# HGRN2 block scores on the tensor engine: two products of 64 keys by 64 queries in the two column halves of the array, in place of one of 128 by 128

## The chip, the cores and the metric

The kernel runs on one core of one Trainium2 chip. A core has five engines that run side by side and wait for each other through semaphores: the tensor engine (PE, with its weight loads listed as PEld), the vector engine (DVE), the scalar engine (ACT), GpSimd (POOL) and the sync engine (SP), whose queue issues most of the transfers from memory. Matrix products read SBUF and write PSUM, where a tile of this kernel is one bank (2 KB in each of 128 partitions). The metric is the device time of one execution in microseconds, smaller being better.

## What is computed

One decoder layer on 256 tokens of width 1024 in float32. One input projection feeds two token mixers, HGRN2 (a gated linear recurrence) and MoBA attention; their outputs are merged by gates and projected, and a SwiGLU feed-forward follows, each with a residual and a layer norm. The change is in HGRN2, which for each of 8 heads computes

```python
log_f = jnp.logaddexp(jnp.log(lb), jnp.log1p(-lb) + jax.nn.log_sigmoid(z))
k = (1.0 - lb) * jax.nn.sigmoid(-z)
...
diff = G[:, :, :, None, :] - G[:, :, None, :, :]          # G = cumsum of log_f
decay = jnp.exp(jnp.where(causal, diff, -jnp.inf))
scores = jnp.einsum('bhtsd,bhtd,bhsd->bhts', decay, qc, kc)
o = jnp.einsum('bhts,bhsv->bhtv', scores, vc) + jnp.einsum('bhtd,bhdv->bhtv', qc * jnp.exp(G), state)
```

The score of a query at token t and a key at token s is a sum over 128 channels d of q, k and the product of the forget gates between s and t, which differs from channel to channel.

## The kernel before

**The levels.** The kernel holds keys and queries with the 128 channels on the partitions and all 256 tokens of 8 heads along the free axis, in two halves `u` of 128 tokens (the second half runs backwards, `ORDER`). It computes the scores in `hgrn_steps` (line 491) by doubling blocks. At level `l` (line 522), with `n = 2**l`, the tokens stand in blocks of `n`, and blocks are paired: a later block of queries against the earlier block of keys beside it. Queries `Qt` and keys `Kt` carry the gates of their blocks already, so a score between the two blocks is a plain product over channels. The views `earlier` (line 485) and `later` (line 488) pick the earlier blocks of keys and the later blocks of queries of both token halves, 128 of each per head.

A level has four parts:

- ACT copies the earlier keys of all 8 heads into the contiguous tile `KL` (line 535; the pool `klp` has one buffer, so the copy for the next level waits until the products of this one have read it).
- PE multiplies, for each head, 128 keys by 128 queries into PSUM (line 543), four heads to a bank, two banks `sc{l}_{g}` a level. The operands are float32, and each such product runs as two matmul instructions with a weight load each: 16 matmul instructions a level. Of the 128 by 128 scores only those between a block and its own partner are wanted. The rest is computed and dropped.
- For blocks under 32 tokens (levels 1 to 4) DVE copies the wanted scores under a mask into `SD` (line 554), once per bank. For blocks of 32 and 64 tokens (levels 5 and 6, `n >= BLOCKS`) ACT copies the wanted rectangles (line 551), 8 copies at level 5 and 4 at level 6.
- DVE multiplies queries (line 560) and keys (line 561) by the gates of the neighbouring block for the next level, and halves the table of gate products (line 564).

Level 0 is different: a product of one key by one query is a sum over partitions, made with a matrix of ones (line 540). It is left as it is. After level 6 come the products between the two token halves (line 572), and then the outputs (line 584).

**What runs around them.** The levels are one step list, `side`, that is advanced between the projections of `hg`, `mv` and `gb` (`tok_chunk`, lines 387 to 389). Each half of such a projection uses one weight tile of 1 MB: SP issues its load (line 220), ACT rounds it (`wh`, line 221), DVE takes the rest (`wl`, line 223), and PE multiplies it in 24 matmuls. There are four buffers each of `wh` and `wl`.

**The order.** In this part of the kernel the order on each engine is not written out: a planner simulates the program and places each instruction when its inputs are ready by its own estimate of times (`schedule_with_timeline_sim=True`, line 1149). Only the start (line 411), the stretch around the output projection (line 903) and the end (line 976) are in an order written out by hand. An engine executes its instructions in the planned order and waits at one whose input isn't there.

Of the kernel before, what the change touches and what calls it, by code (L numbers as in the profile page):

```python
# [10 lines left out]
F32 = mybir.dt.float32  # L11
# [6 lines left out]
P = 128  # L18
T = 256
NT = T // P  # L20
D = 1024
KC = D // P
H = 8
# [103 lines left out]
def hybrid_layer_kernel(ctx: ExitStack, tc, x, xw, vecs, bias, wts, ln1_w, ln1_b, ln2_w, ln2_b, consts, out):  # L127
    nc = tc.nc
# [9 lines left out]
    aux = pool("aux", 4, space=PSUM)  # L138
# [4 lines left out]
    def r32(ap):  # L143
        return ap.bitcast(F32)
# [152 lines left out]
    masks = cst[:, C_MASK:C_END].bitcast(U32).rearrange("p (l t) -> p l t", l=LEVELS)  # L297
# [158 lines left out]
    for j in range(4):  # L456
        sg = sm.tile([P, 2, T], F32, tag="sg", name=f"sgq{j}")
        sgs = [by_half(sg[:, f, :]) for f in range(2)]
        if j < HQ_WIDE:
            for f, ps in enumerate(wide_pair(f"hq{j}", xp, mm, "mm")):  # L460
                z = Qg[:, :, 2 * j + f, :]
# [3 lines left out]
        else:  # L465
            ps = feat_pair(f"hq{j}")
            nc.scalar.activation(sg, ps, AF.Sigmoid)
            qs = [by_half(ps[:, f, :]) for f in range(2)]
        for f in range(2):
            h = 2 * j + f  # L470
# [9 lines left out]
    def free_view(ap, offset, dims):  # L480
        return bass.AP(ap.tensor, ap.offset + offset, [ap.ap[0]] + dims)
# [6 lines left out]
    def later(z, n, h0=0, nh=H):  # L488
        return free_view(z, h0 * P + n, [[P, nh], [2 * n, 64 // n], [H * P - n, NT], [1, n]])

    def hgrn_steps():
        Qt, SD = halves(slot("Qt")), halves(slot("SD"))
        Tt = slot("Tt")
        nc.vector.tensor_mul(Qt, Qg, Fg)


        up, down = slice(0, P // 2), slice(P // 2, P)
        kq, half_sum, kqp = slot("kq"), slot("hs"), slot("kqp", F32R)

        def fold(dst, src, cols, a, b):  # L500

            s = half_sum[a, cols]
            nc.scalar.copy(s, src[b, :])
            nc.vector.tensor_add(s, src[a, :], s)
            nc.scalar.copy(dst[a, :], s)
            nc.vector.tensor_sub(dst[b, :], s, r32(dst[a, :]))

        flat = lambda z: z.rearrange("p u h t -> p (u h t)")
        nc.vector.tensor_mul(kq, flat(Kt), flat(Qg))
        fold(kqp, kq, slice(0, 2048), up, down)  # L510
        yield
        for g in range(4):
            ps = aux.tile([P, 4, P], F32, tag="aux", name=f"sd{g}")
            cs = slice(g * 512, (g + 1) * 512)
            row = ps.rearrange("p h t -> p (h t)")
            nc.tensor.matmul(row, ones, kqp[:, cs], start=True, stop=True)
            nc.vector.tensor_tensor(SD[:, g // 2, 4 * (g % 2):4 * (g % 2) + 4, :], ps,
                                    ident[:, None, :].to_broadcast([P, 4, P]), op=ALU.mult)
        yield
        tot, size = Fg, NT * H * P  # L520
        off = 0
        for l in range(LEVELS):
            n = 2 ** l
            nb = 64 // n
            flat = lambda z: z.rearrange("p h b u i -> p (h b) u i")
            if l == 0:

                pr = klp.tile([P, H * P], F32, tag="kl", name="pr")
                prp = slot("prp", F32R)[:, 0:H * P]
                nc.vector.tensor_mul(pr.rearrange("p (a u i) -> p a u i", u=NT, i=n),  # L530
                                     flat(later(Qt, n)), flat(earlier(Kt, n)))
                fold(prp, pr, slice(0, H * P), down, up)
            else:
                KL = klp.tile([P, H, P], F32, tag="kl", name=f"kl{l}")
                nc.scalar.copy(KL.rearrange("p h (b u i) -> p h b u i", u=NT, i=n), earlier(Kt, n))
            for g in range(2):
                ps = aux.tile([P, 4, P], F32, tag="aux", name=f"sc{l}_{g}")
                if l == 0:
                    row, cs = ps.rearrange("p h t -> p (h t)"), slice(g * 512, (g + 1) * 512)
                    nc.tensor.matmul(row, ones, prp[:, cs], start=True, stop=True)  # L540
                for a in range(4 if l > 0 else 0):
                    h = 4 * g + a
                    nc.tensor.matmul(ps[:, a, :], KL[:, h, :], later(Qt, n, h, 1), start=True, stop=True)  # L543
                if n >= BLOCKS:

                    for b in range(nb):
                        for u in range(NT):
                            r0 = (2 * b + u) * n
                            c0 = 2 * b * n + (1 - u) * n
                            rows = slice(r0, r0 + n)  # L550
                            nc.scalar.copy(SD[rows, u, 4 * g:4 * g + 4, c0:c0 + n], ps[rows, :, r0:r0 + n])
                    continue
                m = masks[:, l, :].rearrange("p (b u i) -> p b u i", u=NT, i=n)
                nc.vector.copy_predicated(later(SD, n, 4 * g, 4),
                                          m[:, None, :, :, :].to_broadcast([P, 4, nb, NT, n]),
                                          ps.rearrange("p a (b u i) -> p a b u i", u=NT, i=n))

            first = free_view(tot, 0, [[2, H * nb], [size // NT + 1, NT], [0, n]])
            second = free_view(tot, 1, [[2, H * nb], [size // NT - 1, NT], [0, n]])
            nc.vector.tensor_mul(flat(later(Qt, n)), flat(later(Qt, n)), first)  # L560
            nc.vector.tensor_mul(flat(earlier(Kt, n)), flat(earlier(Kt, n)), second)
            if l < LEVELS - 1:
                nxt = Tt[:, off:off + size // 2]
                nc.vector.tensor_mul(nxt, free_view(tot, 0, [[2, size // 2]]), free_view(tot, 1, [[2, size // 2]]))
                off += size // 2
                tot, size = nxt, size // 2
            yield
        SL = klp.tile([P, H, P], F32, tag="kl", name="SL")
        for g in range(2):
            ps = aux.tile([P, 4, P], F32, tag="aux", name=f"sc7_{g}")  # L570
            for a in range(4):
                nc.tensor.matmul(ps[:, a, :], Kt[:, 0, 4 * g + a, :], Qt[:, 1, 4 * g + a, :], start=True, stop=True)
            nc.scalar.copy(SL[:, 4 * g:4 * g + 4, :], ps)
        yield
        on = slot("on").rearrange("p (t d) -> p t d", t=NT)
        for g in range(2):
            for u in range(NT):
                ps = aux.tile([P, 4, P], F32, tag="aux", name=f"o{g}{u}")
                for a in range(4):
                    h = 4 * g + a  # L580
                    hd = slice(h * P, (h + 1) * P)
                    if u == 1:
                        nc.tensor.matmul(ps[:, a, :], SL[:, h, :], hv[:, 0, hd], start=True, stop=False)
                    nc.tensor.matmul(ps[:, a, :], SD[:, u, h, :], hv[:, u, hd], start=(u == 0), stop=True)
                sq = sm.tile([P, 4, P], F32, tag="sg", name=f"sq{g}{u}")
                nc.scalar.activation(sq, ps, AF.Square)
                st = sm.tile([P, 12], F32, tag="ost", name=f"ost{g}{u}")
                nc.vector.reduce_sum(st[:, 0:4], sq, axis=mybir.AxisListType.X)
                nc.vector.tensor_scalar(st[:, 4:8], st[:, 0:4], 1.0 / P, RMS_EPS, op0=ALU.mult, op1=ALU.add)  # L589
                nc.gpsimd.tensor_tensor(st[:, 8:12], st[:, 4:8], half, op=ALU.pow)  # L590
                for a in range(4):
                    hd = slice((4 * g + a) * P, (4 * g + a + 1) * P)
                    nc.vector.scalar_tensor_tensor(on[:, u, hd], ps[:, a, :], st[:, 8 + a:9 + a], hgs[:, u, hd],
                                                   op0=ALU.mult, op1=ALU.mult)
            yield
            for j in range(2):
                h0 = 4 * g + 2 * j
                pt = aux.tile([P, 2, T], F32, tag="aux", name=f"ot{g}{j}")
                for a in range(2):
                    for u in range(NT):  # L600
                        hd = slice((h0 + a) * P, (h0 + a + 1) * P)
                        nc.tensor.transpose(pt[:, a, u * P:(u + 1) * P], on[:, u, hd], ident)
                for a in range(2):
                    h = h0 + a
                    nc.scalar.activation(yah[:, h, :], pt[:, a, :], AF.Copy, scale=nw[:, h:h + 1])
                    nc.vector.scalar_tensor_tensor(yal[:, h, :], pt[:, a, :], nw[:, h:h + 1], r32(yah[:, h, :]),
                                                   op0=ALU.mult, op1=ALU.subtract)
        yield
# [367 lines left out]
    with tc.manual_schedule(engines={ET.PE, ET.DVE, ET.Activation}):  # L976
# [56 lines left out]
        z, spare = [slot("z")[:, i:i + D] for i in (0, D)]  # L1033
# [8 lines left out]
        for i, (raw, (k0, wh, wl)) in enumerate(zip(last_raw, held)):  # L1042
# [5 lines left out]
            c = sums[:, 2 * i:2 * i + 2].unsqueeze(2).to_broadcast([P, 2, SUMS])  # L1048
# [106 lines left out]
```

## Time and profile before

| | |
|---|---|
| runs of the kernel (3) | 492.78, 493.17, 493.47 us; median 493.17 us |
| span of the profiled execution, first to last instruction | 491.2 us |
| instructions in the span | 6768 |
| mean granted clock of the tensor engine | 0.996 |
| data moved | 99.99 MB, mean 204 GB/s |
| products of the six levels (line 543) | 96 matmul instructions, first start at 91.0 us, last at 135.6 us |

The span is that of one execution taken by the hardware profiler. No time of its own is listed for that execution outside the profile, so the span stands for it: the 2.0 us between it and the median of the runs lie around the first and the last instruction. In rows of a timeline, the first two numbers are the start and the length in microseconds; in rows of groups, `xN` is the number of instructions, followed by the busy time in us and the mean of one in ns. A matmul's length contains its way through the array, so neighbouring matmuls overlap in time; the pace is read from the distance between starts.

### The profile page before, as it was taken

What the parts mean: (1) busy time and instruction counts of PE and PEld (TensorE: products, weight loads), DVE (VectorE), ACT (ScalarE), POOL (GpSimd) and SP (SyncE); (2) the same over time, 40 slices, a digit from 0 to 9 for tenths busy, and PEclk for the clock granted to TensorE, in tenths of its full rate; (3) what the DMA queues carried; (4) which work ended last, traced back from release to release, by engine and by line L of the source; (5) the groups of instructions that cost most, each with busy time, mean ns of one, the idle gap of its engine ahead of it and who ended that gap; (6) DMA issues with size and microseconds to landing.
All of it is one profiled execution on the core that took longest, in us unless ns stands there. A gap on an engine that the chain in (4) does not pass through costs nothing.

```text
span 491.2 us, 6768 instructions
## 1 busy us (share of the span) xinstructions
PE 484.2 (99%) x2621; PEld 418.4 (85%) x2621; DVE 406.7 (83%) x523; ACT 293.7 (60%) x410; POOL 39.6 (8%) x46
## 2 busy tenths in 40 slices
PE   9999999999999999999999999999999999999994
PEld 9889888888899888988888888888888888888784
DVE  4979899999767979999675678856797878989996
ACT  5797587435755767775843462544655655576673
POOL 0000000000003431250000000000000000000030
PEclk9999999999999999999999999999999999999998
DMA  8987426635442437248545446257869644266852
GB/s 301 418 312 251 172 95 248 229 157 171 172 171 87 131 135 293 107 154 292 220 163 183 168 183 230 103 180 275 314 218 335 218 173 173 90 233 243 315 149 85
DMA packets 17631, 99.99 MB, mean 204 GB/s; under 512 B 1984, under 2 KB 3776, under 8 KB 7616
## 3 DMA queue, kind: packets, MB, share of 16 engines
q1 hardware_dynamic: 14400, 92.62, 51.6%
q0 software_dynamic: 3056, 6.82, 4.3%
q8 instruction: 20, 0.33, 0.3%
q10 hardware_dynamic: 144, 0.13, 0.1%
q14 instruction: 11, 0.09, 0.1%
HBM read 94.84 MB, written 3.15 MB: 199 GB/s over the span
## 4 chain that ended last, share of the span: by engine, by line
PE 90%; DVE 5%; issue 2%; ACT 1%; DMA 1%; DVEq 0%; POOLq 0%; POOL 0%; ACTq 0%
PE fu L336 7%; PE fg L336 7%; PE fg L338 3%; PE fu L338 3%; PE mq L336 2%; PE mk L336 2%; PE hq L336 2%; PE sc L543 2%; PE hf L361 2%; PE za L387 1%; PE ga L387 1%; PE za L388 1%; PE ga L388 1%; PE ga L389 1%; PE za L389 1%
## 5 line engine op out<-in xcount | busy, mean ns | idle before, releaser
L223 DVE TENSOR_TENSOR wl<-raw,wh 128x2048 fp32r<-128x2048 f32 (+1 forms) x71 | 164.9, 2328 | 47.4 <-ACT wh L221 46.9
L221 ACT CAST wh<-raw 128x2048 fp32r<-128x2048 f32 (+1 forms) x71 | 133.6, 1887 | 64.4 <-PE fg L336 13.5
L336 PE MATMUL fg<-x1p,wh 128*128 128x512 f32 x144 | 50.5, 394 | 0.0
L336 PE MATMUL fu<-x1p,wh 128*128 128x512 f32 x144 | 50.4, 394 | 0.0
L338 PE MATMUL fg<-x1p,wl 128*128 128x256 f32 x144 | 40.0, 278 | 0.0
L338 PE MATMUL fu<-x1p,wl 128*128 128x256 f32 x144 | 39.9, 277 | 0.0
L336 PEld LDWEIGHTS fu<-x1p,wh 128*128 128x128 f32 x144 | 27.0, 187 | 6.2
L336 PEld LDWEIGHTS fg<-x1p,wh 128*128 128x128 f32 x144 | 27.0, 187 | 6.1
L338 PEld LDWEIGHTS fg<-x1p,wl 128*128 128x128 f32 x144 | 27.1, 188 | 0.1
L338 PEld LDWEIGHTS fu<-x1p,wl 128*128 128x128 f32 x144 | 27.1, 188 | 0.0
L336 PE MATMUL mk<-xp,wh 128*128 128x512 f32 x48 | 16.8, 396 | 0.0
L336 PE MATMUL mq<-xp,wh 128*128 128x512 f32 x48 | 16.7, 395 | 0.0
L336 PE MATMUL hq<-xp,wh 128*128 128x512 f32 x48 | 16.7, 394 | 0.0
L590 POOL TENSOR_TENSOR ost<-ost,half 128x4 f32<-128x4 f32 x4 | 4.1, 1014 | 152.6 <-DVE ost L589 152.6
L338 PE MATMUL hq<-xp,wl 128*128 128x256 f32 x48 | 13.3, 277 | 0.0
L338 PE MATMUL mq<-xp,wl 128*128 128x256 f32 x48 | 13.0, 279 | 0.0
L338 PE MATMUL mk<-xp,wl 128*128 128x256 f32 x48 | 13.0, 281 | 0.0
L389 PE MATMUL za<-wl,yah 128*128 128x512 f32 x32 | 12.7, 396 | 0.0
L885 PE MATMUL fe<-wh,x1p 128*128 128x512 f32 x32 | 12.6, 395 | 0.0
L387 PE MATMUL za<-wh,yah 128*128 128x512 f32 x32 | 12.6, 395 | 0.0
L389 PE MATMUL gb<-wl,xp 128*128 128x512 f32 x32 | 12.6, 395 | 0.0
L811 PE MATMUL wo<-wh,mTh 128*128 128x512 f32 x32 | 12.6, 394 | 0.0
(380 smaller groups left out, 1359.5 us busy)
## 6 DMA issues: line engine op xcount, KB each, us to landing
raw<-in_wts_dram SPq DMA_DIRECT2D x69, 1024.0 KB, 4.8
rawcorners<-in_wts_dram SPq DMA_DIRECT2D x5, 1024.0 KB, 4.7
xw<-in_xw_dram SPq DMA_DIRECT2D x6, 640.0 KB, 9.6
rawahead<-in_wts_dram SPq DMA_DIRECT2D x2, 1024.0 KB, 4.8
rawsums<-spill SPq DMA_DIRECT2D x2, 1024.0 KB, 4.7
rawcorners<-in_wts_dram SPq DMA_DIRECT2D x2, 768.0 KB, 5.7
raw<-in_wts_dram SPq DMA_DIRECT2D x2, 512.0 KB, 10.8
xr<-in_x_dram POOLq DMA_DIRECT2D x1, 1024.0 KB, 5.5
```

What stands on the lines that cost most here:

```text
L221: nc.scalar.copy(h[:, ks, :], raw[:, ks, :])
L223: eng.tensor_sub(l[:, ks, :], raw[:, ks, :], r32(h[:, ks, :]))
L336: nc.tensor.matmul(ps, wh[:, k, wcol], a.both(k), start=(k == 0), stop=False)
L338: nc.tensor.matmul(ps[:, 0, :], wl[:, k, wcol], a[0, k, slice(0, T)], start=False, stop=(k == KC - 1))
L361: nc.tensor.matmul(ps, wh[:, kk, wcol], xp.both(k), start=False, stop=False)
L387: nc.tensor.matmul(pss[t], ah[:, kk, ts], wh[:, k, :], start=(kk == 0), stop=False)
L388: nc.tensor.matmul(pss[t], al[:, kk, ts], wh[:, k, :], start=False, stop=False)
L389: nc.tensor.matmul(pss[t], ah[:, kk, ts], wl[:, k, :], start=False, stop=(kk == KC - 1))
L543: nc.tensor.matmul(ps[:, a, :], KL[:, h, :], later(Qt, n, h, 1), start=True, stop=True)
L590: nc.gpsimd.tensor_tensor(st[:, 8:12], st[:, 4:8], half, op=ALU.pow)
L811: nc.tensor.matmul(ps, lh(kk)[:, ts], wh[:, k, ns], start=(kk == first), stop=False)
L885: nc.tensor.matmul(ps, x1p[0, kk, ts], wh[:, k, :], start=(kk == 0), stop=False)
```

## The change

For levels 1 to 6, each head's product of 128 keys by 128 queries is replaced by two products of 64 keys by 64 queries: the keys of one half of `KL`'s columns against the queries that belong to them. The first writes PSUM partitions 0 to 63, the second partitions 64 to 127, of a tile with 64 columns a head, so that the scores of all eight heads lie in one bank in place of two. A block and its partner always lie in the same half (for 64 tokens the half is the token half), so every wanted score is still computed. A level has 32 matmul instructions in place of 16, each with 64 weight columns in place of 128 and 64 moving columns in place of 128.

The masked copy of levels 1 to 4 becomes one instruction for 8 heads in place of two for 4 each; it reads the 64 columns twice, once for each half, under the same mask. The copies of levels 5 and 6 take 8 heads at a time: 4 and 2 in place of 8 and 4. Level 0 keeps two banks and two masked copies.

```diff
+    def later_half(z, n, h, c):
+        if n == 64:
+            return free_view(z, h * P + n + c * (H * P - n), [[1, n]])
+        return free_view(z, h * P + n + c * 64, [[2 * n, 32 // n], [H * P - n, NT], [1, n]])
...
-            for g in range(2):
-                ps = aux.tile([P, 4, P], F32, tag="aux", name=f"sc{l}_{g}")
-                if l == 0:
+            m = masks[:, l, :]
+            if l == 0:
+                for g in range(2):
+                    ps = aux.tile([P, 4, P], F32, tag="aux", name=f"sc{l}_{g}")
                     row, cs = ps.rearrange("p h t -> p (h t)"), slice(g * 512, (g + 1) * 512)
                     nc.tensor.matmul(row, ones, prp[:, cs], start=True, stop=True)
-                for a in range(4 if l > 0 else 0):
-                    h = 4 * g + a
-                    nc.tensor.matmul(ps[:, a, :], KL[:, h, :], later(Qt, n, h, 1), start=True, stop=True)
+                    nc.vector.copy_predicated(later(SD, n, 4 * g, 4),
...
+            else:
+                ps = aux.tile([P, H, 64], F32, tag="aux", name=f"sc{l}")
+                for h in range(H):
+                    for c in range(2):
+                        own = slice(c * 64, (c + 1) * 64)
+                        nc.tensor.matmul(ps[own, h, :], KL[:, h, own], later_half(Qt, n, h, c),
+                                         start=True, stop=True)
                 if n >= BLOCKS:
...
-                            nc.scalar.copy(SD[rows, u, 4 * g:4 * g + 4, c0:c0 + n], ps[rows, :, r0:r0 + n])
-                    continue
-                m = masks[:, l, :].rearrange("p (b u i) -> p b u i", u=NT, i=n)
-                nc.vector.copy_predicated(later(SD, n, 4 * g, 4),
-                                          m[:, None, :, :, :].to_broadcast([P, 4, nb, NT, n]),
-                                          ps.rearrange("p a (b u i) -> p a b u i", u=NT, i=n))
+                            nc.scalar.copy(SD[rows, u, :, c0:c0 + n], ps[rows, :, r0 % 64:r0 % 64 + n])
+                else:
+                    part = [[2 * n, 32 // n], [n, NT], [1, n]]
+                    nc.vector.copy_predicated(
+                        free_view(SD, n, [[P, H], [64, 2], [2 * n, 32 // n], [H * P - n, NT], [1, n]]),
+                        free_view(m, 0, [[0, H], [64, 2]] + part),
+                        free_view(ps, 0, [[64, H], [0, 2]] + part))
```

More of the change, by code (lines that the diff above doesn't have):

```diff
@@ L535, in hgrn_steps @@
                 nc.scalar.copy(KL.rearrange("p h (b u i) -> p h b u i", u=NT, i=n), earlier(Kt, n))
-            for g in range(2):
-                ps = aux.tile([P, 4, P], F32, tag="aux", name=f"sc{l}_{g}")
-                if l == 0:
+            m = masks[:, l, :]
+            if l == 0:
+                for g in range(2):
+                    ps = aux.tile([P, 4, P], F32, tag="aux", name=f"sc{l}_{g}")
                     row, cs = ps.rearrange("p h t -> p (h t)"), slice(g * 512, (g + 1) * 512)
                     nc.tensor.matmul(row, ones, prp[:, cs], start=True, stop=True)
-                for a in range(4 if l > 0 else 0):
-                    h = 4 * g + a
-                    nc.tensor.matmul(ps[:, a, :], KL[:, h, :], later(Qt, n, h, 1), start=True, stop=True)
+                    nc.vector.copy_predicated(later(SD, n, 4 * g, 4),
+                                              m.rearrange("p (b u i) -> p b u i", u=NT, i=n)[:, None, :, :, :]
+                                              .to_broadcast([P, 4, nb, NT, n]),
+                                              ps.rearrange("p a (b u i) -> p a b u i", u=NT, i=n))
+            else:
[5 more added lines that the diff above has]
+                                         start=True, stop=True)
                 if n >= BLOCKS:
```

## The prediction

> **What bounds the kernel now.** I read the page first: the busy shares, the forty slices, then the chain that ended last.
>
> ```profile
> span 491.2 us, 6768 instructions
> ...
> PE 484.2 (99%) x2621; PEld 418.4 (85%) x2621; DVE 406.7 (83%) x523; ACT 293.7 (60%) x410; POOL 39.6 (8%) x46
> ...
> PE   9999999999999999999999999999999999999994
> ...
> DVE  4979899999767979999675678856797878989996
> ...
> PE 90%; DVE 5%; issue 2%; ACT 1%; DMA 1%; DVEq 0%; POOLq 0%; POOL 0%; ACTq 0%
> ```
>
> PE is busy in every slice but the last, and the chain runs over PE for 90% of the span. DVE is as full as PE in slices 6 to 10 (61 to 123 us), which is where the levels are worked out. So I look at the levels by stage: the windows view, cut at the products of levels 2 to 6. The columns are the window, its length, then busy time and count for PE, PEld, DVE, ACT and POOL.
>
> ```profile
> 87.50:102.50 15.00, 15.00 (x83) 13.00 (x83) 14.93 (x14) 6.10 (x6) 0.00 (x0) 1.00 0.62 224
> 102.50:110.60 8.10, 8.10 (x45) 6.88 (x44) 8.00 (x7) 3.46 (x4) 0.00 (x0) 1.00 0.34 131
> 110.60:118.80 8.20, 8.20 (x46) 7.08 (x45) 8.10 (x8) 5.18 (x5) 0.00 (x0) 1.00 0.37 128
> 118.80:127.00 8.20, 8.20 (x46) 7.09 (x45) 7.24 (x8) 3.80 (x4) 0.00 (x0) 1.00 0.72 256
> 127.00:136.00 9.00, 9.00 (x50) 7.74 (x49) 6.14 (x5) 7.15 (x16) 0.00 (x0) 1.00 0.34 118
> ```
>
> PE never idles here; DVE idles 0.3 us up to 118.8 and 3.8 us after. The chain of waits for this stretch (start, length) has the six groups of products:
>
> ```profile
> 91.14 1.92 PE sc L543 x16
> ...
> 100.56 1.78 PE sc L543 x16
> ...
> 108.70 1.84 PE sc L543 x16
> ...
> 116.91 1.78 PE sc L543 x16
> ...
> 125.05 1.78 PE sc L543 x16
> ...
> 134.11 1.78 PE sc L543 x16
> ```
>
> All six are on the chain: 1.92 + 1.84 + 4 x 1.78 = 10.88 us, or 0.111 us for each of 16 instructions at 1.78. The change works on these 10.88 us.
>
> **What the products will cost.** A level gets 32 instructions, each with half the queries. What an instruction of 64 columns costs is seen only at the very start, in the timeline of the warm-up products:
>
> ```profile
> 3.26 0.63 PE L430 MATMUL warm<-const-float32-1.0 128*128 128x128 f32 x2
> ...
> 3.47 0.63 PE L430 MATMUL warm<-const-float32-1.0 128*128 128x128 f32 x2
> ...
> 3.90 0.53 PE L430 MATMUL warm<-const-float32-1.0 128*128 128x64 f32 x2
> 4.00 0.42 PE L430 MATMUL warm<-const-float32-1.0 128*128 128x64 f32 x1
> ```
>
> Starts of 128 columns are 0.21 us apart, those of 64 columns 0.10: half. (The pace of these rows is half that of the levels, 0.111, though the clock column shows 1.00 for them; I use the ratio only.) So 64 columns should take 0.111 / 2 = 0.056 us in the levels, and two products of 64 by 64, one after the other, take what one of 128 by 128 takes: 32 x 0.056 = 1.78 us. **Half the columns alone bring nothing; the gain must come from the two halves of the array working at once.** The ends for a group are
>
> - 0.89 us, if the halves overlap completely (32 x 0.028);
> - 1.78 us, if they don't overlap;
> - 3.5 us, if an instruction with its weight load can't be had faster than 0.109 us, which is the least distance that any row at full pace shows (32 x 0.109); the warm-up rows speak only down to 0.10.
>
> The 0.109 is that of the transposes, by the chain:
>
> ```profile
> 275.80 0.87 PE mt L778 x8
> ```
>
> No row has two products in two halves. The order written in the loop is: half 0 first pass, half 0 second pass, half 1 first pass, half 1 second pass, next head. The two passes of one half can't overlap, neighbours of different halves may. If the later of two neighbours starts a step s after the earlier, a head takes 2 x 0.056 + 2 s, with s between 0 and 0.056. The nearest row, the warm-up, shows columns alone setting the pace, so I stay near that end and take a quarter of the way, s = 0.014: 0.139 us a head, 1.11 us a group. Gain: 10.88 - 6 x 1.11 = **4.2 us** (ends: +5.5 and -10.1; the last is 10.88 - 6 x 3.5).
>
> The Trainium skill's page "TensorEngine Tiling (Array Packing)", section "Tiling Modes", says that different tiles of the array can load weights and multiply in parallel, which is what the gain needs. The page "TensorE: Matmul & The Clock Gate", Part 1, section "Wait — 56ns, not 53.3ns?", speaks against it: starts of matmuls never come closer than about 25 ns. With s = 0.025 a head would take 0.161 us, by an estimate from that page, and the gain would be 3.1 us; no row here has starts that close.
>
> **What the change of shape costs.** All products around the levels use the whole array, so each level now enters and leaves another shape: 12 changes. Before, entering and leaving a group is free:
>
> ```profile
> 124.66 0.39 PE L389 MATMUL gb<-wl,xp 128*128 128x512 f32 x1
> ...
> 124.89 1.95 PE L543 MATMUL sc<-Qt,kl 128*128 128x128 f32 x16
> ...
> 126.59 0.48 PE L387 MATMUL gb<-wh,xp 128*128 128x512 f32 x1
> 126.91 0.40 PE L388 MATMUL gb<-wh,xp 128*128 128x512 f32 x1
> ```
>
> From 124.66 to 126.91 are 2.25 us; two products of 512 take 0.23 each, which leaves 1.79 for the 16. The groups by form say what would show if the array had to run empty between two shapes:
>
> ```profile
> L543 PE MATMUL sc<-Qt,kl 128*128 128x128 f32 x96 | 11.9, 276 | 0.0
> ```
> ```profile
> L543 PEld LDWEIGHTS sc<-Qt,kl x96: 186/192/192, 90.7 to 135.5; 128*128 128x128 f32 x96
> ```
>
> An instruction is 0.276 us long at a pace of 0.111: 0.165 us are its way through, hidden by the next one. Running empty exposes these 0.165 us; a weight load that can't start early adds up to 0.19 us. Ends per change: 0 and 0.36 us. I take 0.165, as the load needs nothing from the array's outputs: 12 x 0.165 = **2.0 us** (0 to 4.3). The same page on tiling says, in "Key Properties", that changing the mode drains the array while changing the tile within a mode doesn't. No row of this trace has a change of shape.
>
> **What is late next.** Of the inputs of a group, the queries come last. From the timeline, DVE's multiply and the first product behind it, levels 2 and 3:
>
> ```profile
> 98.37 1.48 DVE L560 TENSOR_TENSOR Qt<-Qt,Tt 128x1024 f32<-128x1024 f32 x1
> ...
> 100.40 0.27 PE L543 MATMUL sc<-Qt,kl 128*128 128x128 f32 x1
> ```
> ```profile
> 107.17 1.21 DVE L560 TENSOR_TENSOR Qt<-Qt,Tt 128x1024 f32<-128x1024 f32 x1
> ...
> 108.54 0.33 PE L543 MATMUL sc<-Qt,kl 128*128 128x128 f32 x1
> ```
>
> The queries are ready 0.55 us before level 2 and 0.16 us before level 3. DVE is full until then and won't be earlier, while PE comes earlier by (4.2 - 2.0) / 6 = 0.37 us a level: 0.37 at level 2, covered; 0.74 at level 3, of which 0.58 isn't. Behind the waiting product the rest of PE's queue waits. The planner places products by its own times and may put another projection product ahead of them. Ends: 0 and 0.6 us (1.6 with full overlap); I take **0.4 us**. Levels 4 and 6 have 2 us in hand (114.92 against 116.91; for level 6 the keys' copy comes last, 131.66 against 133.94):
>
> ```profile
> 113.71 1.21 DVE L560 TENSOR_TENSOR Qt<-Qt,Tt 128x1024 f32<-128x1024 f32 x1
> ```
> ```profile
> 130.61 1.05 ACT L535 COPY kl<-Kt 128x1024 f32<-128x1024 f32 x1
> ...
> 133.94 1.95 PE L543 MATMUL sc<-Qt,kl 128*128 128x128 f32 x16
> ```
>
>
> Can the weights follow? ACT takes a `wh` buffer as PE frees it:
>
> ```profile
> 116.94 1.91 ACT L221 CAST wh<-raw 128x2048 fp32r<-128x2048 f32 x1 [3.02 <-PE gb L388]
> ```
> ```profile
> 120.55 2.28 DVE L223 TENSOR_TENSOR wl<-raw,wh 128x2048 fp32r<-128x2048 f32 x1
> ```
>
> The buffer freed at 116.9 is complete at 122.8, and PE has three other tiles (24 products of 0.23, 5.5 us each) to go through first: over 10 us in hand, so nothing of a gain of 2 to 5 us is lost there, and SP's loads move with the buffers.
>
> **The copies.** The masked ones, with the least, median and greatest length, and ACT's commoner form:
>
> ```profile
> L554 DVE COPY_PREDICATED SD<-cst,sc x10: 733/744/2527, 91.6 to 118.8; 128x512 f32<-128x512 uint32 x10
> ```
> ```profile
> L551 ACT COPY SD<-sc 32x128 f32<-32x128 f32 x8 | 2.0, 255 | 0.1
> ```
>
> Eight masked copies become four of twice the size: the same elements, four starts fewer, counted as nothing (a few tenths on a full DVE). If the new views went at the pace of level 0's copies (2.5 us for 512 elements, the greatest length), each would take 5 us; this is the upper end, and would push the queries back by some 3 us a level, a cost that case 4 below covers. ACT saves under 1 us, and in the windows above it is busy for 25.7 of 48.5 us: nothing.
>
> **Where the gain arrives.** Near the end DVE carries the chain, but it starts from PE:
>
> ```profile
> 443.91 0.24 PE wp L813
> 444.21 1.92 ACT whsums L266
> ```
>
> So whatever PE gains before 444 us moves the end. Sum on the span: -4.2 + 2.0 + 0.4 = -1.8 us, so 489.4 in place of 491.2. The median of the runs lies 2.0 us above the span; the same difference on it gives 491.4 us.
>
> **The rivals.**
>
> 1. Forecast, 0.43: overlap with a small step, 491.4 us. For it: columns set the pace in every row. Full overlap with free changes would be 10.88 - 5.34 = 5.5 us less, 487.6.
> 2. Overlap eaten up, 0.22: with s half of 0.056 a head takes 0.167 us, a group 1.34, the gain is 2.9; changes of shape take 2.0 and the wait 0.2: -0.7 us, 492.5. It is the rule of the 25 ns that leads here.
> 3. Slower, 0.24: the halves don't work at once, the group stays at 1.78 us, and 12 changes at 0.165 to 0.36 us come on top: +2.0 to +4.3 us, 495.2 to 497.5. The place is the first product behind each change. It decides as soon as a group's gain is under two changes, 0.33 us, so above 1.48 us a group. For it: no row shows overlap, and PE has no idle in which a change could hide. It is also the case in which the change doesn't do what it says.
> 4. Much slower, 0.11: 0.109 us per instruction with its weight load, 32 a level: +10.1 + 2.0 us, 505 us. For it: no row at full pace is faster. Against it: the warm-up halves.
>
> **How the numbers follow.** A measurement of this kernel can tell about 0.2% (1 us) from no change. Case 1 is faster by more (0.43), case 2 within (0.22), cases 3 and 4 slower (0.35). The range has to hold cases 1 to 3 with their unknown ends; case 4 and the last half microsecond at either outer end are left out: 488.0 to 497.0 us. Case 1 by itself spans 488 to 492.
>
> **What would show it.** In the profile after: the chain's groups of line 543 at about 1.1 us for 32 instructions (case 3: 1.8; case 4: 3.5); starts of products in different halves closer than 0.056 us; the first product behind a group late by about 0.17 us at either end; PE idle before level 3 by up to 0.6 us with the queries as releaser; masked copies of levels 3 and 4 near 1.4 us each. The forecast is wrong if the groups don't shrink, if a change of shape costs over 0.35 us, or if the planner's new order leaves PE waiting elsewhere.

## The result and the profile after

The changed kernel takes 490.13 us (median of 4 runs, 489.95 to 490.37) against 493.14 us before: a ratio of 0.9942 with a 95% interval of 0.9928 to 0.9956. It is **3.0 us faster**; 491.4 us (1.8 us faster) was predicted. Two single runs, one of the kernel before at 1258 us and one of the kernel with an extra product at the end of each group at 1249 us, lie far outside all the others and are left out of every ratio in this document. The span of the profiled execution went from 491.2 to 488.5 us.

The page of the changed kernel, busy times and the chain's shares:

```profile
span 488.5 us, 6947 instructions
...
PE 481.0 (98%) x2717; PEld 413.0 (85%) x2717; DVE 404.2 (83%) x519; ACT 292.7 (60%) x404; POOL 38.8 (8%) x46
...
PE 89%; DVE 5%; DMA 2%; issue 2%; ACT 1%; DVEq 0%; POOLq 0%; POOL 0%; SPq 0%; ACTq 0%
```

PE has 96 instructions more (six levels, 16 more each) and is busy 3.2 us less. The picture is the old one otherwise: PE carries the chain. The chain of waits (start, length) shows the six groups, now line 556:

```profile
91.34 1.15 PE sc L556 x32
...
100.66 1.08 PE sc L556 x32
101.74 0.43 PE mv L389
...
108.76 1.08 PE sc L556 x32
109.85 0.43 PE mv L389
...
116.87 1.08 PE sc L556 x32
117.95 0.43 PE gb L389
...
126.56 1.08 PE sc L556 x32
127.65 0.43 PE gb L387
...
134.44 1.08 PE sc L556 x32
```

32 instructions take 1.08 us where 16 took 1.78, and the projection product behind a group takes 0.43 us on the chain in place of 0.23. To see both at once, read a group from the last projection product before it to the second one behind it, in the timeline of the changed kernel:

```profile
116.48 0.39 PE L388 MATMUL gb<-wh,xp 128*128 128x512 f32 x1
116.80 1.15 PE L556 MATMUL sc<-Qt,kl 128*64 128x64 f32 x32
117.88 0.50 PE L389 MATMUL gb<-wl,xp 128*128 128x512 f32 x1
118.22 0.39 PE L387 MATMUL gb<-wh,xp 128*128 128x512 f32 x1
```

From 116.48 to 118.22 are 1.74 us; two projection products take 0.23 each (0.46), which leaves **1.28 us** for a group with its two changes of shape. The same reading gave 1.79 before. Six times 0.51 is 3.1 us, the whole gain; read one by one, the six groups save 0.51 to 0.58 us each, 3.2 us together. All experiments below are read in this way; the number is called the group's net time.

### The profile page after: what moved, and what is told of

Its sections match the earlier page's. It is cut to its first block, busy times and chain, and to the rows that moved or that the text cites. A ratio compares the mean times of both kernels' runs of the same rounds, so it can differ in the third digit from the quotient of the medians.

```text
span 488.5 us, 6947 instructions
## 1 busy us (share of the span) xinstructions
PE 481.0 (98%) x2717; PEld 413.0 (85%) x2717; DVE 404.2 (83%) x519; ACT 292.7 (60%) x404; POOL 38.8 (8%) x46
## 4 chain that ended last, share of the span: by engine, by line
PE 89%; DVE 5%; DMA 2%; issue 2%; ACT 1%; DVEq 0%; POOLq 0%; POOL 0%; SPq 0%; ACTq 0%
PE fu L336 7%; PE fg L336 7%; PE fg L338 3%; PE fu L338 3%; PE mq L336 2%; PE mk L336 2%; PE hq L336 2%; PE mv L389 2%; PE gb L389 2%; PE gb L387 2%; PE hg L387 2%; PE hf L361 2%; PE za L387 2%; PE ga L389 2%; PE ga L387 1%
## 5 line engine op out<-in xcount | busy, mean ns | idle before, releaser
L223 DVE TENSOR_TENSOR wl<-raw,wh 128x2048 fp32r<-128x2048 f32 (+1 forms) x71 | 163.2, 2305 | 44.3 <-ACT wh L221 43.9
L389 PE MATMUL mv<-wl,xp 128*128 128x512 f32 x32 | 12.8, 399 | 0.0
```

The costliest lines, as they stand in the source:

```text
L223: eng.tensor_sub(l[:, ks, :], raw[:, ks, :], r32(h[:, ks, :]))
L389: nc.tensor.matmul(pss[t], ah[:, kk, ts], wl[:, k, :], start=False, stop=(kk == KC - 1))
```

## The experiments

Eight kernels were run. Each is the changed kernel with one edit. Ratios are to the kernel before, which ran beside them.

### Do the two halves really work at once?

Half the columns alone were predicted to bring nothing. To see whether the gain comes from the halves working side by side, the same 32 instructions are issued with neighbours in the same half:

```diff
-                for h in range(H):
-                    for c in range(2):
+                for c in range(2):
+                    for h in range(H):
```

PE's instructions, by line and shape, come in the same order as in the changed kernel, so the order inside the groups is all that differs on PE.

> Same instructions as the changed kernel, but within a level all eight products of the left half come first, then all eight of the right half, so neighbours are in the same half. Overlap theory (the gain comes from neighbours in different halves): starts 0.055 us apart throughout, a group of 32 takes 1.75 to 1.8 us in place of 0.94, plus the same two changes of shape: 490.1 + 6 x 0.83 = 495.1 us, slower than the kernel before. Rival (an instruction with 64 weight columns and 64 moving columns simply costs 0.029 us with its load, whichever half it is in): no change, 490.1 us.

Measured: 494.52 us, ratio 1.0026 (1.0017 to 1.0035), slower than before. Its timeline:

```profile
118.34 0.39 PE L388 MATMUL gb<-wh,xp 128*128 128x512 f32 x1
118.66 1.90 PE L556 MATMUL sc<-Qt,kl 128*64 128x64 f32 x32
120.49 0.50 PE L389 MATMUL gb<-wl,xp 128*128 128x512 f32 x1
120.82 0.39 PE L387 MATMUL gb<-wh,xp 128*128 128x512 f32 x1
```

2.48 - 0.46 = 2.02 us net, 0.74 more than in the changed kernel; six times that is 4.4 us, and the time rose by 4.4 us. The rival (narrow instructions are cheap wherever they stand) is out. A product's half of the array is also its half of the PSUM partitions; no run separates the two. This run is also the price of the prediction's third case: without alternating halves the change would have cost 1.3 us, less than the 2.0 to 4.3 named there, since at the one border the halves still overlap a little.

### How far can a later product run ahead?

The prediction assumed that instructions start strictly in order, so that only neighbours in different halves overlap. Two orders between the extremes test it. The edit is that of two heads in a row; for four heads, the 2 of the step and the 2 of the inner loop are 4:

```diff
-                for h in range(H):
-                    for c in range(2):
-                        own = slice(c * 64, (c + 1) * 64)
...
+                for h, c in [(h0 + a, c) for h0 in range(0, H, 2) for c in range(2) for a in range(2)]:
+                    own = slice(c * 64, (c + 1) * 64)
```

> The changed kernel's products with two heads in a row in the same half: left half heads 0 and 1, right half heads 0 and 1, and so on, so runs of 4 instructions in one half. Strictly in order, only the neighbours at the 7 borders overlap: 32 x 0.0585 - 7 x 0.052 = 1.51 us a group (0.94 with single products), +0.57 a level, 493.5 us. If a later instruction of the other half can start while earlier ones still wait for theirs (in the kernel that takes the halves in turn, three instructions overlap at the one border), three of four overlap at each border: 32 x 0.0585 - 21 x 0.052 = 0.78, so no less than the 0.94 of full overlap, 490.1 us.

> The same with four heads in a row in the same half: runs of 8 instructions, 3 borders. Strictly in order: 32 x 0.0585 - 3 x 0.052 = 1.72 us a group, +0.78 a level, 494.8 us. If three instructions overlap at each border: 1.40 us a group, +0.46 a level, 492.9 us.

Measured: 490.65 us with two heads in a row (ratio 0.9948, 0.9929 to 0.9968), 492.35 us with four (0.9978, 0.9967 to 0.9989). The timelines, two heads in a row and then four:

```profile
116.97 0.39 PE L388 MATMUL gb<-wh,xp 128*128 128x512 f32 x1
117.29 1.20 PE L555 MATMUL sc<-Qt,kl 128*64 128x64 f32 x32
118.42 0.50 PE L389 MATMUL gb<-wl,xp 128*128 128x512 f32 x1
118.76 0.39 PE L387 MATMUL gb<-wh,xp 128*128 128x512 f32 x1
```
```profile
117.59 0.39 PE L388 MATMUL gb<-wh,xp 128*128 128x512 f32 x1
117.90 1.54 PE L555 MATMUL sc<-Qt,kl 128*64 128x64 f32 x32
119.38 0.50 PE L389 MATMUL gb<-wl,xp 128*128 128x512 f32 x1
119.71 0.40 PE L387 MATMUL gb<-wh,xp 128*128 128x512 f32 x1
```

Net 1.33 and 1.66 us. Less 0.35 for the two changes (next experiment) these are 0.98 and 1.31 us of products, below the strict order's 1.51 and 1.72 and beside the other theory's 0.94 and 1.40. The built programs hold the products of a group in the order written. So an instruction of the other half starts while a few before it still wait for theirs. Runs of 4 instructions in one half are nearly free, runs of 8 are not.

### Products and changes of shape, each by itself

Issuing every product of a level twice leaves the two changes as they are and doubles the rest:

```diff
-                for h in range(H):
+                for h in list(range(H)) * 2:
```

> Each level's 16 products are issued twice in a row, 64 instructions between one entry and one exit. If a group is 0.94 us of products (16 neighbours pairs of 0.0585) plus a fixed 0.34 us for entering and leaving the other shape: +0.94 us a level, 490.1 + 5.6 = 495.7 us, and the extra time at the two ends of the group stays as it is. Rival without fixed cost (1.28 us / 32 = 0.040 us an instruction): +1.28 us a level, 497.8 us.

Measured: 496.06 us, ratio 1.0054 (1.0037 to 1.0071).

```profile
117.95 0.39 PE L388 MATMUL gb<-wh,xp 128*128 128x512 f32 x1
118.27 2.08 PE L556 MATMUL sc<-Qt,kl 128*64 128x64 f32 x64
120.28 0.50 PE L389 MATMUL gb<-wl,xp 128*128 128x512 f32 x1
120.62 0.39 PE L387 MATMUL gb<-wh,xp 128*128 128x512 f32 x1
```

2.67 - 0.46 = 2.21 us net for 64 instructions against 1.28 for 32: **0.93 us for 32 instructions, and 0.35 us that don't depend on their number.** The second term by another way: an extra product of 128 by 128 in the middle of a group brings two changes more, the same product at its end none.

```diff
+                wide = aux.tile([P, P], F32, tag="aux", name=f"wide{l}")
                 for h in range(H):
+                    if h == 4:
+                        nc.tensor.matmul(wide, KL[:, h, :], later(Qt, n, h, 1), start=True, stop=True)
```

> The changed kernel with one extra product of 128 keys by 128 queries a level (two instructions, 0.22 us, its result isn't used), put between head 3 and head 4 of each group, so that each level leaves and enters the other shape once more: two more changes a level. If a change costs 0.17 us: +6 x (0.22 + 0.34) = +3.4, 493.5 us, and the instruction behind each change is late as at the ends of the group. If a change costs nothing of itself: +1.3, 491.4 us, the same as with the extra product at the end.

> The changed kernel with the same extra product of 128 keys by 128 queries a level (its result isn't used) behind head 7, where the shape changes anyway: no more changes than before. Both theories: +6 x 0.22 = +1.3, 491.4 us. It is what the kernel with the product in the middle is to be compared with.

Measured: 494.38 us (ratio 1.0029, 1.0020 to 1.0039) in the middle, 492.08 us (0.9982, 0.9972 to 0.9993) at the end. Timelines, middle and end:

```profile
117.61 0.39 PE L389 MATMUL gb<-wl,xp 128*128 128x512 f32 x1
117.93 0.69 PE L559 MATMUL sc<-Qt,kl 128*64 128x64 f32 x16
118.55 0.49 PE L556 MATMUL wide<-Qt,kl 128*128 128x128 f32 x2
118.97 0.69 PE L559 MATMUL sc<-Qt,kl 128*64 128x64 f32 x16
119.58 0.50 PE L387 MATMUL gb<-wh,xp 128*128 128x512 f32 x1
119.92 0.39 PE L388 MATMUL gb<-wh,xp 128*128 128x512 f32 x1
```
```profile
116.67 0.39 PE L388 MATMUL gb<-wh,xp 128*128 128x512 f32 x1
116.99 1.15 PE L557 MATMUL sc<-Qt,kl 128*64 128x64 f32 x32
118.07 0.49 PE L559 MATMUL wide<-Qt,kl 128*128 128x128 f32 x2
118.31 0.48 PE L389 MATMUL gb<-wl,xp 128*128 128x512 f32 x1
118.63 0.39 PE L387 MATMUL gb<-wh,xp 128*128 128x512 f32 x1
```

Net 1.85 and 1.50 us: two changes cost 0.35 us, 0.17 each, and the time differs by 2.3 us where six times 0.35 is 2.1. The product at the end costs 1.50 - 1.28 = 0.22 us a level, as expected, which is 1.3 us; the run was 2.0 us above the changed kernel. The other 0.6 us isn't in the groups and stays open; apart from the one left out, the runs of this kernel lay between 491.2 and 492.8 us.

### Is it the products, or the merged copies?

The changed products with the old copies: two banks of four heads, a masked copy for each, 8 and 4 copies by ACT.

```diff
-                ps = aux.tile([P, H, 64], F32, tag="aux", name=f"sc{l}")
+                for g in range(2):
+                    ps = aux.tile([P, 4, 64], F32, tag="aux", name=f"sc{l}_{g}")
...
-                            nc.scalar.copy(SD[rows, u, :, c0:c0 + n], ps[rows, :, r0 % 64:r0 % 64 + n])
+                                nc.scalar.copy(SD[rows, u, hs, c0:c0 + n], ps[rows, :, r0 % 64:r0 % 64 + n])
...
-                        free_view(SD, n, [[P, H], [64, 2], [2 * n, 32 // n], [H * P - n, NT], [1, n]]),
+                            free_view(SD, 4 * g * P + n, [[P, 4], [64, 2], [2 * n, 32 // n], [H * P - n, NT], [1, n]]),
```

> The changed kernel's products, but scores in two banks of four heads each, with two masked copies a level (4 heads each) and 8 and 4 copies by the scalar engine, as in the kernel before. If the gain is the products' alone: 490.1 us within 0.6. Rival (the merged copies free the vector engine and bring the queries of levels 2 and 3 earlier): PE waits before level 3 by up to 0.6 us, or the planner moves the groups back, 490.7 us and more.

Measured: 490.28 us, ratio 0.9940 (0.9925 to 0.9955), the changed kernel's time. The merged copies bring nothing that can be measured; the interval is about 0.7 us wide to either side. But here the predicted wait exists, in the timeline of PE and DVE at level 3:

```profile
106.99 0.39 PE L389 MATMUL mv<-wl,xp 128*128 128x512 f32 x1
107.67 1.15 PE L558 MATMUL sc<-Qt,kl 128*64 128x64 f32 x32 [0.30 <-DVE Qt L576]
```
```profile
106.32 1.21 DVE L576 TENSOR_TENSOR Qt<-Qt,Tt 128x1024 f32<-128x1024 f32 x1
```

PE stands idle for 0.30 us until the queries are there at 107.53. In the changed kernel they are ready 0.49 us ahead:

```profile
107.00 1.20 DVE L575 TENSOR_TENSOR Qt<-Qt,Tt 128x1024 f32<-128x1024 f32 x1
...
108.69 0.28 PE L556 MATMUL sc<-Qt,kl 128*64 128x64 f32 x2
```

The planner moved work there: between the first products of levels 2 and 3 lie 8.1 us in both kernels (100.59 to 108.69 after, 100.40 to 108.54 before), though the group in between is 0.5 us shorter. In the trace, 30 projection products lie between these two points in place of 28. With two banks the planner puts only 25 there, so PE arrives too early although the queries are ready earlier too (107.53 against 108.20).

### Four quarters in place of two halves

For blocks of up to 16 tokens, a pair of blocks fits into 32 columns. Levels 1 to 4 as four products of 32 keys by 32 queries, levels 5 and 6 in halves:

```diff
+    def later_quarter(z, n, h, c):
+        return free_view(z, h * P + n + c * 32, [[2 * n, 16 // n], [H * P - n, NT], [1, n]])
...
+                w = 32 if n < BLOCKS else 64
                 for h in range(H):
-                    for c in range(2):
-                        own = slice(c * 64, (c + 1) * 64)
-                        nc.tensor.matmul(ps[own, h, :], KL[:, h, own], later_half(Qt, n, h, c),
-                                         start=True, stop=True)
+                    for c in range(P // w):
+                        own = slice(c * w, (c + 1) * w)
+                        q = later_quarter(Qt, n, h, c) if w == 32 else later_half(Qt, n, h, c)
+                        nc.tensor.matmul(ps[own, h, 0:w], KL[:, h, own], q, start=True, stop=True)
...
-                    part = [[2 * n, 32 // n], [n, NT], [1, n]]
+                    part = [[2 * n, 16 // n], [n, NT], [1, n]]
...
-                        free_view(SD, n, [[P, H], [64, 2], [2 * n, 32 // n], [H * P - n, NT], [1, n]]),
-                        free_view(m, 0, [[0, H], [64, 2]] + part),
-                        free_view(ps, 0, [[64, H], [0, 2]] + part))
+                        free_view(SD, n, [[P, H], [32, 4], [2 * n, 16 // n], [H * P - n, NT], [1, n]]),
+                        free_view(m, 0, [[0, H], [32, 4]] + part),
+                        free_view(ps, 0, [[64, H], [0, 4]] + part))
```

> Levels 1 to 4 as four products of 32 keys by 32 queries in the four column quarters, 64 instructions a level; levels 5 and 6 in halves as before. If a product costs its first pass plus a start step of 0.006 us (two passes of one product can't overlap, neighbours in different quarters do): 0.028 + 0.006 = 0.034 us a product, 0.135 us a head against 0.117, +0.15 us a level, 490.7 us. Rival 1 (columns alone set the pace): the group halves to 0.47 us, 488.2 us. Rival 2 (an instruction with its load can't be had under the 0.029 us it has now): 1.88 us a group, +0.94 a level, 493.9 us.

Measured: **488.83 us**, ratio 0.9909 (0.9895 to 0.9924), the fastest of all kernels here. The timeline of PE at levels 4 and 3:

```profile
115.57 0.39 PE L389 MATMUL gb<-wl,xp 128*128 128x512 f32 x1
115.89 0.76 PE L561 MATMUL sc<-Qt,kl 128*32 128x32 f32 x64
116.58 0.50 PE L387 MATMUL gb<-wh,xp 128*128 128x512 f32 x1
116.92 0.40 PE L388 MATMUL gb<-wh,xp 128*128 128x512 f32 x1
```
```profile
108.18 0.75 PE L561 MATMUL sc<-Qt,kl 128*32 128x32 f32 x64 [0.24 <-DVE Qt L579]
```

The group has 1.35 - 0.46 = 0.89 us net. Its 64 starts lie in 0.57 us (from 115.888 to 116.455), 0.009 us apart on average. Less the 0.35 measured with halves for two changes of shape, 0.54 us of the net time would be products; what the changes cost with quarters was not measured. The first theory's expectation (1.08 us, slower by 0.6) was wrong, for the same reason as the step s: it took the starts to be strictly in order. Columns alone would give 0.47 and 488.2 us, about 0.1 a group away. Level 3 here has the wait for the queries again, 0.24 us.

## Why the prediction was right, and where its sizes were off

- **The place and the mechanism** were right. The gain is the six groups' (six times 0.51 = 3.1 us), it needs the overlap of the halves, and without it the change loses 1.3 us.
- **The products: the term that was mis-sized.** Predicted 1.11 us a group, a gain of 4.2; measured 0.93, a gain of 10.88 - 6 x 0.93 = 5.3. The step s was taken as 0.014 us between strictly ordered starts. The runs of two and four heads show that the order isn't strict, and in the changed kernel 0.93 us for 32 instructions is 0.029 each. Inside one half, where the halves are taken one after the other, starts are 0.058 us apart (the fourth at 118.88, the ninth at 119.17). Half of that is 0.029, so the overlap is complete. The 0.04 us a group above the predicted end of 0.89 comes from the pace, 0.058 in place of the 0.056 that the ratio of the warm-up rows gave.
- **The changes of shape: the size was right, the reason only in part.** Predicted were 0.165 us each, from the way through the array; 0.17 was measured in two ways, 2.1 us in all. The prediction counted the weight load at nothing, as if it could start early. In the trace it doesn't. Before, the first weight load of a group starts 0.22 us ahead of its product at 124.89. In the changed kernel the first load behind either change starts together with its product, at 116.80 and at 117.88; the weight loads of the kernel before, then of the changed one:

```profile
124.67 0.41 PEld L543 LDWEIGHTS sc<-Qt,kl 128*128 128x128 f32 x2
```
```profile
116.80 1.01 PEld L556 LDWEIGHTS sc<-Qt,kl 128*64 128x64 f32 x32 [0.35 <-issue]
117.88 0.19 PEld L389 LDWEIGHTS gb<-wl,xp 128*128 128x128 f32 x1
```

The first two products of the group are 0.27 us long, the others 0.22. So a late load is probably part of the 0.17; how much of it is the load and how much the array running empty, no run separates. If the load is part of it, the agreement with 0.165 is partly luck. The Trainium skill's page "TensorEngine Tiling (Array Packing)", section "Tiling Modes", says that a change of mode drains the array; the runs show a cost of 0.17 us at each change, but not how much of it is draining.
- **The wait for the queries** was predicted at 0.4 us and is 0 in the changed kernel. The mechanism exists (0.30 us with two banks, 0.24 us with quarters), but in this kernel the planner's order covers it.
- **The copies** were counted as nothing, which the kernel with two banks confirms within the spread of the runs (490.28 against 490.13 us). The masked copies of 8 heads are 1.31 us long (median of four, the longest 2.46), near the 1.4 forecast and under the upper end of 5.
- **Arrival at the end:** in the chain of the changed kernel ACT's work that takes over from PE near the end starts 2.85 us earlier than before (444.21 us), and the gain shows in the runs nearly in full:

```profile
441.36 1.92 ACT whsums L266
```

- **The second rival** went by the Trainium skill's page "TensorE: Matmul & The Clock Gate", section "Wait — 56ns, not 53.3ns?", with its 25 ns between starts. The runs differ: 32 starts lie in 0.93 us (1.15 less the 0.22 of the last), in pairs about 0.01 us apart, and with quarters 64 starts lie in 0.57 us, 0.009 us apart on average. The measurement decides: the distance does not hold where neighbours stand in different columns of the array. The fourth rival's 0.109 us an instruction is out by the same rows.
- **Slips in the working,** without weight for the forecast: the second rival's gain is 10.88 - 6 x 1.34 = 2.8 us, not 2.9; the wait's end with full overlap is 1.7 us (twice 0.92 less 0.16), not 1.6; and 0.109 us is the least pace of equal products, while single starts come closer: the projection product at 126.59 starts 0.03 us behind the last of the group before it (126.56).

The sum with measured terms: -5.3 + 2.1 + 0 = -3.2 us, where the runs gained 3.0. The predicted sum was -1.8; of the 1.4 us between them, 1.1 are the products and 0.4 the wait, less 0.1 for the changes of shape.

## What to carry to other kernels

Where a product computes a block-diagonal result and drops the rest, cut it into column parts of the array and let neighbours alternate between the parts: the products' time fell nearly with the number of parts here (1.79, 0.93 and about 0.55 us for one, two and four), as long as the order alternates. Two products in a row in one part cost 0.05 us a group, four cost 0.38 of the 0.51 saved, and eight lost it all. Count 0.17 us for each change between this shape and the full array, so put the small products in one group: a group of 16 instructions saved 0.86 us and paid 0.35 for it. When PE gets faster, look at the input that comes last before each group: whether it turns into a wait was decided here by the planned order, not by the products.

## What the runs showed that was not expected

- A later product for another part of the array can start ahead of a few waiting ones: with runs of 4 instructions in one half the group took 0.98 us against 1.51 in strict order.
- Four quarters overlap nearly as well as two halves: 64 instructions, each with a weight load of its own, start 0.009 us apart on average, where the full-array products of the same levels before stood 0.111 us apart.
- At a change of shape the weight load, which otherwise runs ahead, starts together with its product: 0.00 us ahead at 116.80, against 0.22 us before.
